# The second matrix of an MLP in seven products of half blocks, in one of three token groups

## The chip, the cores and the metric

The kernel runs on one core of one Trainium2 chip. The metric is the device time of one execution in microseconds (us). Five engines work side by side, each with its own queue of instructions in order, and wait for one another by semaphores: TensorE (PE, matrix products, with PEld for its weight loads), VectorE (DVE), ScalarE (ACT), GpSimd (POOL) and SyncE (SP, which here only issues DMAs; POOL issues DMAs, too).

## The reference

One step of a decoder layer, in float32, for a prompt of 2048 tokens and for 8 samples of 4 tokens:

```
xn  = rms_norm(x, norm_mix_pre);  z = xn @ w_in
y   = concat(mLSTM heads(z), sliding-window attention(z))
x   = x + rms_norm(y @ w_out, norm_mix_post)
u   = rms_norm(x, norm_ffn_pre)
f   = square(relu(u @ w_up)) @ w_down          # 1024 -> 4096 -> 1024
x   = x + rms_norm(f, norm_ffn_post)
x   = x + sigmoid(x @ w_pgate) * (p @ w_pproj)
```

The change concerns `square(relu(u @ w_up)) @ w_down` for a part of the prompt's tokens. The samples' mLSTM and attention ("decode") are a separate piece of work, which reads cached states and keys.

## The kernel before

**Products.** A float32 matrix is held as a pair of tiles, h (rounded) and l (the rest). `mm3` makes a product of three matmuls: h by h, h by l, l by h. Splitting costs a cast on ACT and a subtraction on DVE (`split`) or on DVE and POOL in turn (`wsplit`).

**Groups and steps.** The 16 blocks of 128 tokens form six chunks and three groups of two chunks (`GROUPS`: 6, 6 and 4 blocks). The input projection, the mLSTM and the attention of all blocks come first. Then each group in turn goes through w_out (`mix_mm`, PE name `mo`), the MLP (`mlp`) and the gate (`gate_mm`, `pg` and `pv`). `mlp` cuts the 4096 hidden columns into 16 steps of 256 (FS = 2 halves of 128). Steps 0 and 1 (step 0 alone starts the sums in f) make w_up's product directly (`up`). From step 2 on (`FAST`) `up_both` makes it for both chunks at once in seven products of half blocks instead of eight: it needs sums of the inputs (`sums`, `last_sum`, made during step 1 by DVE and POOL, L1641 to L1675) and differences of the weights (`Ring.product`, L306 to L313), and puts the seven results together on DVE (`add`, L1692). `hidden` then takes relu and square on ACT (L1617, L1618) and splits (L228, L229), giving `hh` and `hl` for each chunk and half.

**w_down.** `down` multiplies the hidden blocks of one chunk with half of w_down's 1024 output columns at a time; a product for one block of tokens takes two halves x three matmuls of 512 columns, in one of three PSUM banks (`ps_mm`, PE name `dn`). DVE adds each finished bank to the sum f in SBUF (L1728). A step has two chunks x two column halves x three blocks: 12 such sums, 72 matmuls. w_up's products go through two other banks (`ps_s`, name `up`).

**The weight ring.** All weight tiles go through one ring of 7 pair tiles (`Ring.pair`, tile name `w`), in the order that `plan` writes out; a tile takes the place of the one seven before it, when that has been used and, if need be, stored. At its first use a weight is loaded raw by SP (`wr`, `wb`), split on ACT (L249) and on DVE or POOL (L250), and, if it is used again, stored in device memory by a DMA that POOL issues (`wk<-w`, L275). Later uses load the stored pair (`w<-wk`, SP). So the first group splits and stores the MLP's weights, and the second and third load them.

**Order.** PE's order is the program's. Side work (decode, transposes, the sums above) is written as generators; each yields a time, and `Flow` continues it when so much matmul time, by its own count, has been written out. `decode` yields `DECW` first, then loads its data through POOL's queue and goes on in pieces between the matmuls of the second group's `mix_mm` and step 0; it is finished (`drain`) before step 1 begins, when its memory on the right side goes to the sums for w_up. The other engines' order is settled by the compiler from the program's order and from what is ready.

## Time and profile before

| what | value |
|---|---|
| runs | 2674.84, 2672.45, 2677.86 us; median 2674.84 |
| profiled execution | 2676.5 us, span in the profile 2674.7 us |
| PE / DVE / ACT / POOL busy | 95% / 55% / 36% / 25% of the span |
| PE's granted clock, mean | 0.981 |
| MLP steps 2 to 13, first group | about 870 to 1267 us of the span |
| MLP steps 2 to 13, second group | about 1600 to 1976 us of the span |
| matmuls of w_down (`dn`) | 1792 with hh, 896 with hl, in all groups |

"Busy" is the time in which an engine works on an instruction. In the chain of work each row is a start, a duration and what ran; in rows of groups, the count follows an x, then come the busy time and the mean in ns of one, and after the second bar the idle time ahead of them with what ended it. In windows, each engine has its busy time and in brackets its count, then come the granted clock, the share of the DMA engines and GB/s. In the order of time, each row is a start, a duration, an engine, a line and an operation.

### The profile page before, as it was taken

The numbers are of one execution on the slowest core, as the hardware profiler recorded it, in microseconds if no ns is written. First come the engines' busy times: TensorE is split into PE (matmuls) and PEld (weight loads), VectorE is DVE, ScalarE is ACT, GpSimd is POOL, SyncE is SP. The second block draws the span as 40 slices with busy tenths as digits, with TensorE's granted clock in tenths as the row PEclk, the third lists the DMA queues.
The fourth block names the chain that finished last, engine by engine and source line by source line (L and its number), as shares of the span: only waits on it lengthen the run. The fifth ranks groups of instructions, "written<-read, shape, count | busy, mean of one in ns | idle before, by whom it ended". The sixth has DMA issues, their size and how long they took to land.

```text
span 2674.7 us, 39114 instructions
## 1 busy us (share of the span) xinstructions
PE 2549.5 (95%) x14260; PEld 2212.9 (83%) x14260; DVE 1481.7 (55%) x3112; ACT 975.9 (36%) x2165; POOL 658.0 (25%) x936
## 2 busy tenths in 40 slices
PE   7899999998899999999998999999999998999998
PEld 6787878877688888888776789988888877999986
DVE  6675666664677655655735564444446345444443
ACT  5545344543455433444513432222223133222231
POOL 5311111111436666666513320000001012000010
PEclk9999999999999999999998999999999998999999
DMA  8765656666786666666987645555557885777786
GB/s 305 268 215 173 217 167 221 210 241 224 255 326 240 254 245 236 236 236 233 341 323 238 209 142 188 189 189 174 173 182 256 288 316 187 254 261 258 257 297 230
DMA packets 215186, 632.23 MB, mean 236 GB/s; under 512 B 24790, under 2 KB 58794, under 8 KB 214977
## 3 DMA queue, kind: packets, MB, share of 16 engines
q1 hardware_dynamic: 169552, 472.19, 52.0%
q0 software_dynamic: 45392, 157.50, 15.1%
q8 instruction: 113, 1.85, 0.3%
q14 instruction: 81, 0.66, 0.1%
q10 hardware_dynamic: 48, 0.03, 0.0%
HBM read 475.47 MB, written 155.25 MB: 236 GB/s over the span
## 4 chain that ended last, share of the span: by engine, by line
PE 74%; DVE 10%; DMA 6%; issue 4%; POOL 3%; ACT 2%; SPq 0%; POOLq 0%; DVEq 0%; ACTq 0%
PE dn L145 20%; PE up L145 20%; PE pg L145 5%; PE mo L145 5%; PE v L145 3%; DMA wk<-w 3%; PE qk L145 2%; DVE hl L229 2%; DMA w<-wk 2%; PE o L145 2%; PE gv L145 2%; PE qa L145 1%; PE aT L149 1%; PE aO L145 1%; PE pv L145 1%
## 5 line engine op out<-in xcount | busy, mean ns | idle before, releaser
L145 PE MATMUL dn<-w,hh 128*128 128x512 f32 x1792 | 566.6, 397 | 13.7 <-DVE f L1449 5.1
L145 PEld LDWEIGHTS dn<-w,hh 128*128 128x128 f32 x1792 | 333.2, 189 | 95.1 <-DVE f L1728 8.6
L1728 DVE TENSOR_TENSOR f<-f,dn 128x512 f32<-128x512 f32 x420 | 286.9, 687 | 222.0 <-PE dn L145 220.9
L145 PE MATMUL dn<-w,hl 128*128 128x512 f32 x896 | 355.5, 397 | 2.5 <-DVE hl L229 2.4
L1692 DVE TENSOR_TENSOR re<-up,re 128x384 f32<-128x384 f32 (+1 forms) x294 | 152.0, 517 | 326.4 <-PE up L145 326.4
L145 PEld LDWEIGHTS dn<-w,hl 128*128 128x128 f32 x896 | 169.0, 189 | 46.3 <-DVE hl L229 7.5
L1693 ACT COPY re<-up 128x384 f32<-128x384 f32 (+1 forms) x42 | 18.9, 450 | 414.8 <-PE up L145 414.8
L1617 ACT ACTIVATE re<-re 128x384 f32<-128x384 f32 (+1 forms) x168 | 83.2, 495 | 207.9 <-DVE re L1692 205.8
L229 DVE TENSOR_TENSOR hl<-re,hh 128x384 fp32r<-128x384 f32 (+1 forms) x192 | 137.7, 717 | 31.1 <-ACT hh L228 30.4
L275 POOL DMA_DIRECT2D wk<-w x242 | 134.0, 555 | 32.2 <-DVE w L250 29.2
L1443 POOL TENSOR_TENSOR f<-f,gffn 128x512 f32<-128x512 f32 x16 | 21.8, 1365 | 476.5 <-ACT j L1441 476.2
L250 POOL TENSOR_TENSOR w<-wr,w 128x512 fp32r<-128x512 f32 (+2 forms) x76 | 104.9, 1380 | 87.5 <-ACT w L249 86.6
L249 ACT CAST w<-wb 128x512 fp32r<-128x512 f32 x98 | 60.7, 621 | 173.2 <-PE dn L145 118.3
L249 ACT CAST w<-wr 128x512 fp32r<-128x512 f32 (+2 forms) x152 | 89.3, 598 | 85.6 <-PE up L145 34.3
L250 POOL TENSOR_TENSOR w<-wb,w 128x512 fp32r<-128x512 f32 x70 | 91.9, 1313 | 116.3 <-ACT w L249 115.8
L1618 ACT ACTIVATE re<-re 128x384 f32<-128x384 f32 (+1 forms) x192 | 95.1, 495 | 5.9
L228 ACT CAST hh<-re 128x384 fp32r<-128x384 f32 (+1 forms) x192 | 92.8, 483 | 6.8
L1043 ACT ACTIVATE s<-s,swt 128x257 f32<-128x257 f32 (+1 forms) x128 | 63.4, 497 | 77.5 <-DVE swt L1040 76.4
L1037 DVE CUSTOM_DVE_ANT_0 s<-aS,cst,sink 128x256 f32<-128x256 f32 (+1 forms) x128 | 57.0, 473 | 59.4 <-PE aS L145 59.2
L1624 POOL CAST hh<-hh 128x16 fp32r<-128x16 f32 x32 | 8.0, 249 | 319.0 <-ACT hh L228 319.0
L145 PE MATMUL up<-t0h,w 128*128 128x384 f32 (+1 forms) x336 | 85.1, 320 | 0.0
L145 PE MATMUL up<-t1h,w 128*128 128x384 f32 (+1 forms) x336 | 85.1, 320 | 0.0
(1537 smaller groups left out, 6530.7 us busy)
## 6 DMA issues: line engine op xcount, KB each, us to landing
w<-wk SPq DMA_DIRECT2D x692, 512.0 KB, 4.7
wk<-w POOLq DMA_DIRECT2D x238, 512.0 KB, 6.6
wr<-in_w_down_dram SPq DMA_DIRECT2D x64, 256.0 KB, 7.7
wb<-in_w_up_dram SPq DMA_DIRECT2D x28, 512.0 KB, 6.8
w<-wk SPq DMA_DIRECT2D x20, 528.0 KB, 4.4
x<-in_x_prompt_dram SPq DMA_DIRECT2D x16, 512.0 KB, 5.2
y<-yd SPq DMA_DIRECT2D x32, 256.0 KB, 7.1
xr<-in_x_prompt_dram SPq DMA_DIRECT2D x16, 512.0 KB, 6.3
```

Source lines behind the costliest of these rows:

```text
L145: ins = self.pe.matmul(out, lhsT, rhs, start=start, stop=stop)
L228: act.copy(hi, src)
L229: dve.tensor_tensor(lo, src, hi.bitcast(F32), ALU.subtract)
L249: act.copy(hi, src)
L250: (eng or weng()).tensor_tensor(lo, src, hi.bitcast(F32), ALU.subtract)
L275: here(put(self.kept[key], t.bitcast(U32)))
L1037: dve.tensor_tensor_reduce(s_[:, s, lo : 2 * P], pS[:, s, lo:], bias[:, j, lo:], 1.0 if s == 0 else 0.0625, sink[:, h : h + 1], ALU.add, A ...
L1043: act.activation(e_, e_, AF.Exp, bias=nm[:, s : s + 1], accum_out=sm[:, s : s + 1])
L1617: act.activation(t, src, AF.Relu)
L1618: act.square(t, t)
L1692: add = lambda out, a, b: dve.tensor_tensor(out, a, b, ALU.add)
L1728: dve.tensor_tensor(out(i), out(i), ps[i], ALU.add)
```

## The change

In the second group (`SGROUP` = 1), steps 2 to 13 (`SEVEN`) go in six pairs. `up_seven` is `up_both` with another end: it names the four hidden blocks A11, A12 (first chunk, halves 1 and 2), A21, A22 (second chunk), and makes on POOL s1 = A21 + A22, s3 = A11 - A21, s2 = s1 - A11 and s4 = A12 - s2. It splits seven operands (A11, A12, A22, s3, s1, s4, s2) instead of four. `down_seven` then makes, for a pair of steps, seven products; in each, a block of 128 tokens sums both steps in one PSUM bank (2 x 3 matmuls), and DVE adds the bank to one or two destinations: quarters of f, or a shared sum U. After the last pair `share` adds U on POOL to three of the four quarters (nine half blocks).

The weights for this are w_down's blocks and four differences of them for each step. They are made in the first group: `Ring.row` with a step collects the four raw blocks, takes four differences on POOL, splits each (ACT and DVE), puts them through the ring and stores them. The second group loads 14 tiles for a pair's w_down instead of 8.

Besides, `DECW` goes from 5 to 20; the raw tiles move to the right side of memory and are given up in the second group's step 1; the pool `wide` (temporaries of the sums for w_up) is given up in step 2 for the operands and U; the pool `sp2` has one buffer instead of two.

```diff
-DECW = 5.0
+DECW = 20.0
...
+SEVEN = range(2, STEPS - 2)
+SGROUP = 1
...
-            self.raw = es.enter_context(tc.tile_pool(name=nm + "raw", bufs=raws))
+            self.raw = es_raw.enter_context(tc.tile_pool(name=nm + "raw", bufs=raws, side="right"))
...
-        def row(self, key, src, n):
+        def row(self, key, src, n, step=None):
             def make(h, l):
                 raw = self.load(n)
                 dma(raw, src)
                 wsplit(h, l, raw)
+                if step is None:
+                    return
+                self.four.append(raw)
+                if len(self.four) < 4:
+                    return
+                b11, b21, b12, b22 = self.four
+                self.four = []
+                sub = lambda out, a, b: pool.tensor_tensor(out, a, b, ALU.subtract)
+                sub(b11, b12, b11)
+                sub(b12, b22, b12)
+                sub(b22, b22, b11)
+                sub(b21, b21, b22)
+                for i, raw in ((1, b11), (3, b12), (2, b22), (4, b21)):
+                    t = self.tile(n)
+                    wsplit(t[:, 0], t[:, 1], raw, dve)
+                    self.keep(("t", step, i), t)
...
+                if gi == SGROUP and s in SEVEN:
+                    if s % 2:
+                        both = s - 1, s
+                        for k in range(FS):
+                            for e in both:
+                                yield row(w_down, e * FS + k, 0)
+                        for i in (3, 4, 1, 0, 2):
+                            for e in both:
+                                yield diff(e, i) if i else row(w_down, e * FS + 1, 1)
+                    continue
+                step = s if gi == 0 and s in SEVEN else None
...
-    sp2 = es2.enter_context(tc.tile_pool(name="sp2", bufs=2, reuse_waits="tile"))
+    sp2 = es2.enter_context(tc.tile_pool(name="sp2", bufs=1, reuse_waits="tile"))
...
+        def up_seven(s, X):
...
+            rectify(t[0], t[0])
+            s1 = wq.tile([P, UW], F32, tag="s1", name=f"s1{nm}")[:, :W]
+            pool.tensor_tensor(s1, t[0], t[2], ALU.add)
+            sub(t[0], t[1], t[0])
+            A["s3"] = parts(hq, t[0], f"{nm}s3")
+            A["s1"] = parts(hq, s1, f"{nm}s1")
+            sub(t[1], s1, t[1])
+            sub(t[3], t[3], t[1])
+            A["s4"] = parts(hq, t[3], f"{nm}s4")
+            A["s2"] = parts(hq, t[1], f"{nm}s2")
+            return A
+
+        def down_seven(s, As, U, first):
+            c0, c1 = chunks
+            def out(ci, half):
+                return lambda i: f[chunks[ci][i]][:, half * 512 : half * 512 + 512]
+            u = lambda i: U[:, i]
+            uses = (
+                ("11", u, out(0, 0)),
+                ("12", out(0, 0)),
+                ("s3", out(1, 1), out(1, 0)),
+                ("22", out(1, 0)),
+                ("s1", out(1, 1), out(0, 1)),
+                ("s4", out(0, 1)),
+                ("s2", u),
+            )
+            for n, (a, *to) in enumerate(uses):
+                w = [[t[:, :512] for t in w] for w in ring.take(2)]
+                for i in range(len(c0)):
+                    ps = psum(ps_mm, f"ds{G}{s}{n}{i}")
+                    for e in range(2):
+                        mm3(ps, [y[:, cols(i)] for y in As[e][a]], w[e], e == 0, e == 1)
+                        pe.tick()
+                    for m, o in enumerate(to):
+                        if first and n == 0 and m == 0:
+                            act.copy(o(i), ps)
+                        else:
+                            dve.tensor_tensor(o(i), o(i), ps, ALU.add)
+
+        def share(U):
+            for ci, half in ((0, 1), (1, 0), (1, 1)):
+                for i, b in enumerate(chunks[ci]):
+                    v = f[b][:, half * 512 : half * 512 + 512]
+                    pool.tensor_tensor(v, v, U[:, i], ALU.add)
...
+            if gi == SGROUP and s in SEVEN:
+                if s == SEVEN[0]:
+                    es_w.close()
...
+                As.append(up_seven(s, X))
+                if len(As) == 2:
+                    down_seven(s, As, U, s == SEVEN[1])
+                    As = []
+                if s == SEVEN[-1]:
+                    share(U)
+                continue
```

More of the change, by code (lines that the diff above doesn't have):

```diff
@@ L281, in get @@
             if key in self.kept:
+                assert all(k != key for _, k, _ in self.later)
                 dma(t.bitcast(U32), self.kept[key])
@@ L386, in hybrid_layer @@
     small = ctx.enter_context(tc.tile_pool(name="small", bufs=6))
-    ring = Ring(ctx, "w", RAWS, PAIRS)
+    es_raw = ExitStack()
+    ring = Ring(ctx, es_raw, "w", RAWS, PAIRS)
     def rows2(k, o, n):
@@ L412, in plan, with row, diff @@
                     )
-        def row(w, k, half):
+        def row(w, k, half, step=None):
             src = w[k * P : (k + 1) * P, half * 512 : half * 512 + 512]
-            return (w.tensor.name, k, half), lambda key: ring.row(key, src, 512)
+            return (w.tensor.name, k, half), lambda key: ring.row(key, src, 512, step)
+        def diff(s, i):
+            return ("t", s, i), lambda key: ring.get(key, 512, None)
         def heads(k, half):
@@ L442, in plan @@
                         yield two(s, q)
+                if gi == SGROUP and s in SEVEN:
[9 more added lines that the diff above has]
+                step = s if gi == 0 and s in SEVEN else None
                 for half in (0, 1, 0, 1) if s == 0 else (0, 1):
                     for k in range(s * FS, (s + 1) * FS):
-                        yield row(w_down, k, half)
+                        yield row(w_down, k, half, step)
             for ci in range(2):
@@ L1612, in up, with parts @@
                 pe.tick()
+        def parts(pool_, t, nm):
+            y = [pool_.tile([P, UW], F32R, tag=f"h{e}", name=f"h{e}{nm}")[:, : t.shape[1]] for e in "hl"]
+            split(*y, t)
+            return y
         def hidden(s, ci, ft, t, src, hid):
@@ L1675, in last_sum, with rectify @@
                 dve.tensor_tensor(l, t3, h.bitcast(F32), ALU.subtract)
-        def up_both(s, X, hid):
+        def rectify(t, src):
+            act.activation(t, src, AF.Relu)
+            act.square(t, t)
+        def up_seven(s, X):
             W = X[0][0].shape[2]
             nm = f"{G}{s}"
+            product = products(s, X)
+            A = {}
+            t = [wq.tile([P, UW], F32, tag="re", name=f"rq{nm}")[:, :W]]
+            t += [wp.tile([P, UW], F32, tag="re", name=f"re{nm}{n}")[:, :W] for n in range(1, 4)]
+            add = lambda out, a, b: dve.tensor_tensor(out, a, b, ALU.add)
+            sub = lambda out, a, b: pool.tensor_tensor(out, a, b, ALU.subtract)
+            act.copy(t[0], product(1))
+            add(t[1], product(2), t[0])
+            rectify(t[1], t[1])
+            A["11"] = parts(hp, t[1], f"{nm}a11")
+            add(t[0], product(6), t[0])
+            add(t[2], product(7), t[0])
+            add(t[3], product(4), t[2])
+            rectify(t[3], t[3])
+            A["12"] = parts(hp, t[3], f"{nm}a12")
+            ps = product(5)
+            add(t[2], ps, t[2])
+            add(t[0], ps, t[0])
+            rectify(t[2], t[2])
+            A["22"] = parts(hp, t[2], f"{nm}a22")
+            add(t[0], product(3), t[0])
+            rectify(t[0], t[0])
[9 more added lines that the diff above has]
+            return A
@@ L1689, in product, with up_both @@
                 return ps
+            return product
+        def up_both(s, X, hid):
+            W = X[0][0].shape[2]
+            nm = f"{G}{s}"
+            product = products(s, X)
             t = [wp.tile([P, UW], F32, tag="re", name=f"re{nm}{n}")[:, :W] for n in range(4)]
@@ L1771, in mlp @@
                 es_lp.close()
+                if gi == SGROUP:
+                    es_raw.close()
                 es_t = ExitStack()
                 tp = es_t.enter_context(tc.tile_pool(name="tp", bufs=1, side="right", reuse_waits="tile"))
[L1774 removed]
+                es_w = ExitStack()
+                ring.wide = es_w.enter_context(tc.tile_pool(name="wide", bufs=WIDE, side="right", reuse_waits="tile"))
                 tsp.add(sums())
+            if gi == SGROUP and s in SEVEN:
+                if s == SEVEN[0]:
+                    es_w.close()
+                    es_w = ExitStack()
+                    hq = es_w.enter_context(tc.tile_pool(name="hq", bufs=6, side="right", reuse_waits="tile"))
+                    wq = es_w.enter_context(tc.tile_pool(name="wq", bufs=2, side="right", reuse_waits="tile"))
+                    U = es_w.enter_context(tc.tile_pool(name="us", bufs=1, side="right", reuse_waits="tile")).tile(
+                        [P, CMAX, 512], F32, name=f"us{G}"
+                    )
+                    As = []
+                As.append(up_seven(s, X))
+                if len(As) == 2:
+                    down_seven(s, As, U, s == SEVEN[1])
+                    As = []
+                if s == SEVEN[-1]:
+                    share(U)
+                continue
             if fast:
```

8 lines of the change are left out of this document (5 added, 3 removed).

## The prediction

> **What bounds the kernel now.** I read the page first, then the chain of work, then windows of one step each, then groups of instructions in the two stretches that the change touches, and last the order of time round single waits.
>
> ```profile
> span 2674.7 us, 39114 instructions
> PE 2549.5 (95%) x14260; PEld 2212.9 (83%) x14260; DVE 1481.7 (55%) x3112; ACT 975.9 (36%) x2165; POOL 658.0 (25%) x936
> ```
>
> TensorE (PE) is the bound as a whole, so fewer matmuls are worth their time wherever PE does not wait already. The chain shows one step of the second group and the distance between two steps of the first; the windows show what the other engines do in such a step.
>
> ```profile
> 1693.73 14.71 PE up L145 x84
> 1708.45 16.72 PE dn L145 x72
> ...
> 1170.89 12.57 PE up L145 x72
> ...
> 1202.89 12.54 PE up L145 x72
> ```
>
> ```profile
> core 0: us, PE busy (x) PEld busy (x) DVE busy (x) ACT busy (x) POOL busy (x), PEclk, DMA share, GB/s
> 1171.00:1203.00 32.00, 31.76 (x158) 28.01 (x157) 19.21 (x28) 13.12 (x25) 20.13 (x23) 1.00 0.64 247
> 1693.73:1725.17 31.44, 31.44 (x158) 28.25 (x157) 14.02 (x23) 6.75 (x13) 0.00 (x0) 1.00 0.57 184
> ```
>
> In the second group a step is 14.71 + 16.72 = 31.4 us, all of it matmul at full clock, with POOL (GpSimd) idle and DVE (VectorE) busy 14.0. There 72 matmuls of w_down take 16.72, so one is 0.232 us, and one of w_up is 14.71 / 84 = 0.175. In the first group the same step takes 1202.89 - 1170.89 = 32.0: PE already loses 0.6, with POOL busy 20.1 and DVE 19.2. These two rows decide the case: the change saves PE time where everything else is idle, and pays with DVE and POOL time where both are busy.
>
> **What the group rows say.** First the stretch 1599 to 2007 (second group), then 883 to 1235 (first group).
>
> ```profile
> L1728 DVE TENSOR_TENSOR f<-f,dn 128x512 f32<-128x512 f32 x156 | 107.4, 688 | 96.3 <-PE dn L145 96.3
> L1692 DVE TENSOR_TENSOR re<-up,re 128x384 f32<-128x384 f32 x91 | 50.7, 557 | 127.6 <-PE up L145 127.6
> L229 DVE TENSOR_TENSOR hl<-re,hh 128x384 fp32r<-128x384 f32 x52 | 28.7, 551 | 2.2 <-ACT hh L228 2.2
> L1618 ACT ACTIVATE re<-re 128x384 f32<-128x384 f32 x52 | 27.4, 526 | 1.6
> L228 ACT CAST hh<-re 128x384 fp32r<-128x384 f32 x52 | 26.8, 515 | 1.7
> ```
>
> ```profile
> L275 POOL DMA_DIRECT2D wk<-w x121 | 66.5, 551 | 16.3 <-DVE w L250 15.8 <-POOL w L250 0.5
> L229 DVE TENSOR_TENSOR hl<-re,hh 128x384 fp32r<-128x384 f32 x44 | 55.9, 1271 | 0.0
> L249 ACT CAST w<-wr 128x512 fp32r<-128x512 f32 x44 | 27.4, 622 | 28.1 <-PE up L145 26.2 <-DMA wk<-w 1.9
> L250 DVE TENSOR_TENSOR w<-wr,w 128x512 fp32r<-128x512 f32 x22 | 15.5, 704 | 2.3 <-ACT w L249 0.6
> L313 POOL TENSOR_TENSOR wb<-wb,wb 128x512 f32<-128x512 f32 x11 | 14.6, 1327 | 16.4 <-DVE w L250 16.4
> L306 POOL TENSOR_TENSOR wb<-wb,wb 128x512 f32<-128x512 f32 x11 | 14.5, 1314 | 1.1 <-DMA wb<-in_w_up_dram 1.1
> ```
>
> The same split of a hidden block (L229) means 0.551 us where POOL is idle and 1.271 where it works. The order of time in one step of the first group says why:
>
> ```profile
> 1119.46 1.31 POOL L307 TENSOR_TENSOR wb<-wb 128x512 f32<-128x512 f32 x1
> 1120.72 1.29 POOL L306 TENSOR_TENSOR wb<-wb,wb 128x512 f32<-128x512 f32 x1
> ```
>
> ```profile
> 1119.85 2.58 DVE L229 TENSOR_TENSOR hl<-re,hh 128x384 fp32r<-128x384 f32 x1
> ```
>
> The DVE split starts inside the first POOL instruction and ends 0.42 after the second, as if it ran only when POOL was through with both. Operations that read PSUM keep their time beside POOL. So a run of POOL instructions holds up a DVE instruction that reads SBUF twice, and everything behind it on DVE.
>
> **The change, part by part.**
>
> *Second group, matmuls.* Six pairs of steps. A pair had 2 x 72 matmuls of w_down and now has 7 products x 3 blocks x 2 steps x 3 = 126: 18 fewer, 108 in all, x 0.232 = -25.1 us. PE has no wait in this stretch, so all of it lies on the path. w_up stays as it is.
>
> *Second group, DVE.* Sums from PSUM grow from 24 to 30 in a pair (+4.1), splits from 8 to 14 (+3.3): 28.0 + 7.4 = 35.4 of some 59. On average it fits; locally it is tight. A product takes PE 18 x 0.232 = 4.18, and one with two destinations takes DVE 6 x 0.688 = 4.13. POOL gets four sums of 128x384 in each step; from 1.31 by width about 1.0 each (an estimate), 3.9 in a run. After the last product of w_up the first new operand (s3) needs a sum (0.56), two activations (1.05), two POOL sums (2.0), a cast (0.52) and a split (0.55): 4.7, or 6.7 if the split waits for POOL's other two. It is used after two products, 8.36 later: hidden, by 1.7. But in those two products DVE has nine sums (6.2), about three splits (1.7) and up to 2.0 of blocking, 9.9 for 8.4, against a cover of two free PSUM banks (2 x 1.39). Ends 0 and 2 us for a pair; nearer to the low one, since products with one destination follow and let DVE catch up: 0.6, x 6 = +3.6. The queue of SP loads 28 tiles for a pair instead of 22, 14.7 MB in 59 us, 250 GB/s, which the windows above show DMA doing in the first group; no cost.
>
> *Second group, the shared sum.* Behind the last pair POOL adds U to nine half blocks.
>
> ```profile
> L1443 POOL TENSOR_TENSOR f<-f,gffn 128x512 f32<-128x512 f32 x16 | 21.8, 1365 | 476.5 <-ACT j L1441 476.2
> ```
>
> 9 x 1.365 = 12.3 us without a break, beside the 14.7 of the next step's w_up; w_down of that step begins after it. A split of that step held up from its start at about 6 until 12.3 keeps the sums behind it, and w_up has two PSUM banks (4.2): ends 0 and 6, I take +3 (the middle; no row shows so long a run).
>
> *First group, twelve steps.* Added in each: four POOL sums (4 x 1.31 = 5.2), four casts on ACT (2.5), four splits on DVE (2.8), four stores issued by POOL (4 x 0.551 = 2.2). POOL goes from 20.1 to 27.5 of 32, DVE from 19.2 to 22.0 before any blocking, stores by 2.1 MB in 32 us, from 247 to about 313 GB/s.
>
> ```profile
> wk<-w POOLq DMA_DIRECT2D x121, 512.0 KB, 7.9
> ```
>
> The four tiles also go through the ring of seven weight tiles. The next step's second tile now takes the place of the third w_down tile, which is free only when the step's last matmul is done; it is wanted one product (12 x 0.175 = 2.1) later, and a cast (0.62) and a split (0.70) need 1.3. Covered by 0.8, unless POOL blocks the split (by 2.0 in the row of 2.58 above). Stores wait in POOL's queue behind its sums, and a tile of the ring is free only when its store has landed, 7.9 after issue; the first w_down tiles take the place of the step's first w_up tiles, stored some 10 us ahead, so this has a cover of about 2. For the sum: below, nothing new reaches PE and a step costs 0.2 more; above, the four POOL sums run without a break, a DVE split waits 5.2 + 0.55, PE's two spare banks cover 2 x 1.39, and a step loses 3.0. A run of two POOL sums goes with the 0.6 lost now; four more make two such runs, so I take 1.1, x 12 = +13.
>
> *Decode starts 15 later.* The waits of PE between 1290 and 1600:
>
> ```profile
> PE dph L149 <- DMA hrow<-in_state_mlstm_conv_dram: 9.0, 1, 9.0
> ...
> PE dn L145 <- ACT hh L228: 2.3, 1, 2.3
> PE dn L145 <- ACT re L1617: 2.3, 1, 2.3
> ```
>
> ```profile
> 1410.00:1420.00 10.00, 6.62 (x26) 5.25 (x27) 5.52 (x22) 1.81 (x3) 5.79 (x10) 0.50 0.26 57
> ```
>
> ```profile
> 1549.02 1.90 PE L145 MATMUL daO<-svc,spts 128*128 128x64 f32 x16
> 1558.28 0.34 PE L145 MATMUL up<-ut10h,w 128*128 128x384 f32 x1
> ```
>
> ```profile
> 1554.59 0.94 DVE L1641 TENSOR_TENSOR ts<-ut11h,ut10h 128x768 f32<-128x768 f32 x1
> ```
>
> Decode's first transposes stand in PE's order before their data: 9.0 of waiting, and a clock of 0.50 behind it: 6.6 us of work at half speed cost about 3 more. Fifteen later in PE's order the data is there if the loads are issued no later: -12. At the other end decode now runs past the start of step 1 (1558.28 against 1549.02 + 15): its last transposes stand without work between them (+1), and the sums for w_up (L1641), which took decode's memory 3.7 us before step 1 began, start about 7 later against PE. They caused the two waits of 2.3; between 0 and 7 more, I take +6 in all. Net -6, between -12 and +3 (loads late, all seven lost).
>
> *Free.* The raw tiles move to the other side of memory and the small pool loses a buffer that the third group uses one at a time; the code shows no wait.
>
> **Sum.** -25.1 + 3.6 + 3 + 13 - 6 = -11.5 against the profiled execution's 2676.5 gives 2665.0; the median of the runs is 1.7 below that execution, so 2663.
>
> **Rivals.** *Slower: POOL in the first group.* Place: the run of four sums and what it does to DVE, with POOL 86% busy. For it: 1.271 against 0.551. Against: stores between the sums let DVE in. At 3.0 a step it is 36 instead of 13: 2686. It decides from (13 + 11.5) / 12 = 2.0 a step.
>
> *Nothing to be seen.* A loss of 2.0 a step in the first group, 24 instead of 13, or the same 11 us lost in the pairs of the second (1.8 each): 2674. For it: DVE with 4.13 in 4.18. Against: its average there is 60%.
>
> *More is kept.* DVE gets in after one POOL instruction instead of after the run. Then no wait exceeds 1.3, the spare banks cover it, the first group pays 0.3 a step (3.6) and the shared sum nothing: 2663 - 9.4 - 3 = 2651. For it:
>
> ```profile
> 1566.90 2.43 POOL L1647 TENSOR_TENSOR ts<-ut11h,ts 128x768 f32<-128x768 f32 x1 [0.96 <-DVE t1l L1659]
> 1569.41 2.44 POOL L1649 TENSOR_TENSOR ts<-ts,ut11l 128x768 f32<-128x768 f32 x1
> ```
>
> ```profile
> 1567.55 2.60 DVE L1659 TENSOR_TENSOR t0l<-ts,t0h 128x768 fp32r<-128x768 f32 x1
> ```
>
> Here the DVE instruction ended at 1570.15, inside the second POOL instruction. Against it: the 2.58 above, where POOL had no gap. [...]
>
> **How the numbers follow.** Forecast 0.46 (own range 2654 to 2669), more kept 0.14, nothing to be seen 0.16, slower 0.24 (the rival 0.20, the rest for a bad decode or DVE). A change under 0.2%, 5.3 us, can't be told from none here. So faster 0.60, same 0.16, slower 0.24. The range from 2646 to 2688 leaves out a tenth at each end: everything kept, and POOL at its worst together with another loss.
>
> **What would show it.** Right: windows of a pair in the second group of 58.7 to 60 instead of 62.8; steps of 33 in the first group with POOL near 27; no wait on hrow; longer waits in step 1. Wrong: waits of PE on f sums or on weights (w) of over 2 us a step in the first group, waits on f sums in the second, or L229 above 2 us in the mean.

## The result and the profile after

Four runs of the changed kernel have a median of 2750.9 us (2744.4 to 2753.7), four of the kernel before on the same chip 2676.4: a ratio of 1.0276, 95% interval 1.0253 to 1.0299. The change costs 2.8%; 2663 was forecast, and the time lies above the range. The profiled execution took 2753.7, its span is 77.2 longer than before's. First the head of the page of the kernel after.

```profile
span 2751.9 us, 39613 instructions
PE 2560.7 (93%) x14152; PEld 2212.2 (80%) x14152; DVE 1602.0 (58%) x3229; ACT 1014.4 (37%) x2252; POOL 807.6 (29%) x1089
```

There are 108 matmuls fewer, and PE is nevertheless busy for 11 us more: behind many waits it runs at a lower clock (0.971 in the mean of the span, 0.981 before). The windows of one step of the first group and one pair of the second:

```profile
core 0: us, PE busy (x) PEld busy (x) DVE busy (x) ACT busy (x) POOL busy (x), PEclk, DMA share, GB/s
1169.20:1206.80 37.60, 34.93 (x163) 29.59 (x161) 25.73 (x32) 15.00 (x29) 28.24 (x30) 0.95 0.72 265
1732.00:1796.93 64.93, 60.55 (x295) 54.05 (x295) 36.33 (x58) 16.17 (x32) 8.53 (x8) 0.97 0.68 226
```

A step of the first group takes 37.6 (32.0 before), with POOL at 28.2 and DVE at 25.7: nothing is full. This pair takes 64.9 (65.2 in the mean of the six, 62.8 before), where the matmuls alone need 58.7. PE's waits, first in the first group's steps (870 to 1310), then in the second's (1660 to 2060); the columns are the total in us, the times, the longest.

```profile
PE up L147 <- ACT w L251: 10.8, 6, 1.8
PE up L147 <- DVE re L1819: 10.1, 5, 3.3
PE dn L147 <- DVE f L1855: 9.2, 10, 1.6
PE dn L147 <- DVE hl L231: 8.2, 4, 4.2
PE up L147 <- POOL w L252: 5.1, 8, 0.7
```

```profile
PE ds L147 <- DVE f L1791: 13.5, 6, 2.2
PE up L147 <- DVE re L1733: 12.8, 6, 2.1
```

From the start of PE's first matmul of each stage, in the order of time, comes the table in which the 77.2 can be placed:

| stage (us) | before | after | difference | forecast |
|---|---|---|---|---|
| first group, steps 2 to 13 | 383.7 | 445.0 | +61.3 | +13 |
| first group, steps 14 and 15 | 75.9 | 80.9 | +5.0 | 0 |
| second group, `mix_mm` (decode's start) | 108.6 | 95.7 | -12.9 | -12 |
| second group, steps 0 and 1 (decode's end) | 92.9 | 104.5 | +11.6 | +6 |
| second group, steps 2 to 13 | 376.8 | 390.9 | +14.1 | -21.5 |
| second group, steps 14 and 15 | 75.7 | 75.6 | -0.1 | +3 |

The rest of the kernel differs by less than 2. Two terms are wrong: the first group by 48, the pairs of the second by 36. Line numbers below are those of the kernel after (L147 matmuls, L231 splits of hidden blocks, L251 and L252 casts and splits of weights, L277 stores, L310 to L316 sums for w_up's weights, L358 the four differences, L1733 and L1791 the second group's sums from PSUM) or, for a variant, of its own text.

### The profile page after: what moved, and what is told of

It reads as the page before. It is cut to its first block, busy times and chain, and to the rows that moved or that the text cites. A ratio compares the mean times of both kernels' runs of the same rounds, so it can differ in the third digit from the quotient of the medians.

```text
span 2751.9 us, 39613 instructions
## 1 busy us (share of the span) xinstructions
PE 2560.7 (93%) x14152; PEld 2212.2 (80%) x14152; DVE 1602.0 (58%) x3229; ACT 1014.4 (37%) x2252; POOL 807.6 (29%) x1089
## 4 chain that ended last, share of the span: by engine, by line
PE 66%; DVE 10%; DMA 7%; POOL 7%; issue 6%; ACT 4%; SPq 0%; POOLq 0%; ACTq 0%; DVEq 0%
PE up L147 16%; PE dn L147 11%; PE ds L147 6%; PE pg L147 5%; PE mo L147 5%; PE v L147 3%; DMA wk<-w 3%; DMA w<-wk 2%; PE qa L147 2%; PE qk L147 2%; POOL w L252 2%; PE gv L147 2%; PE o L147 1%; PE aT L151 1%; PE aO L147 1%
## 5 line engine op out<-in xcount | busy, mean ns | idle before, releaser
L147 PE MATMUL dn<-w,hh 128*128 128x512 f32 x1216 | 392.8, 405 | 28.3 <-DVE f L1855 12.3
L147 PEld LDWEIGHTS dn<-w,hh 128*128 128x128 f32 x1216 | 227.8, 192 | 89.1 <-DVE f L1855 20.9
L147 PE MATMUL dn<-w,hl 128*128 128x512 f32 x608 | 244.1, 401 | 10.3 <-DVE hl L231 10.1
L1855 DVE TENSOR_TENSOR f<-f,dn 128x512 f32<-128x512 f32 x276 | 184.4, 682 | 82.9 <-PE dn L147 82.6
L277 POOL DMA_DIRECT2D wk<-w x290 | 159.3, 551 | 96.2 <-DVE w L252 86.9
L251 ACT CAST w<-wr 128x512 fp32r<-128x512 f32 (+2 forms) x200 | 117.1, 601 | 170.5 <-DMA wk<-w 64.2
L252 DVE TENSOR_TENSOR w<-wr,w 128x512 fp32r<-128x512 f32 (+2 forms) x124 | 129.8, 1064 | 65.7 <-ACT w L251 65.3
L147 PEld LDWEIGHTS dn<-w,hl 128*128 128x128 f32 x608 | 116.6, 192 | 40.8 <-DVE hl L231 13.7
L231 DVE TENSOR_TENSOR hl<-re,hh 128x384 fp32r<-128x384 f32 (+1 forms) x144 | 109.0, 757 | 42.1 <-ACT hh L230 41.2
L252 POOL TENSOR_TENSOR w<-wr,w 128x512 fp32r<-128x512 f32 (+2 forms) x76 | 99.2, 1306 | 90.3 <-ACT w L251 89.5
L1791 DVE TENSOR_TENSOR f<-f,ds 128x512 f32<-128x512 f32 x144 | 94.4, 684 | 39.4 <-PE ds L147 34.7
L1661 ACT ACTIVATE re<-re 128x384 f32<-128x384 f32 (+1 forms) x120 | 57.8, 481 | 154.2 <-DVE re L1819 152.1
L147 PE MATMUL up<-ut01h,w 128*128 128x384 f32 x288 | 88.4, 374 | 23.8 <-ACT w L251 10.8
L252 POOL TENSOR_TENSOR w<-wb,w 128x512 fp32r<-128x512 f32 x70 | 93.4, 1334 | 26.1 <-ACT w L251 25.3
L147 PE MATMUL up<-ut11h,w 128*128 128x384 f32 x288 | 80.9, 343 | 12.8 <-DVE re L1733 12.8
L1081 ACT ACTIVATE s<-s,swt 128x257 f32<-128x257 f32 (+1 forms) x128 | 63.3, 497 | 76.6 <-DVE swt L1078 75.6
L1075 DVE CUSTOM_DVE_ANT_0 s<-aS,cst,sink 128x256 f32<-128x256 f32 (+1 forms) x128 | 57.0, 473 | 59.0 <-PE aS L147 58.7
L147 PE MATMUL up<-t2h,w 128*128 128x384 f32 (+1 forms) x336 | 87.8, 329 | 1.0 <-DVE re L1819 1.0
```

The source lines that it names most:

```text
L147: ins = self.pe.matmul(out, lhsT, rhs, start=start, stop=stop)
L231: dve.tensor_tensor(lo, src, hi.bitcast(F32), ALU.subtract)
L251: act.copy(hi, src)
L252: (eng or weng()).tensor_tensor(lo, src, hi.bitcast(F32), ALU.subtract)
L277: here(put(self.kept[key], t.bitcast(U32)))
L1075: dve.tensor_tensor_reduce(s_[:, s, lo : 2 * P], pS[:, s, lo:], bias[:, j, lo:], 1.0 if s == 0 else 0.0625, sink[:, h : h + 1], ALU.add, A ...
```

## The experiments

In the runs of a part alone the other parts are as in the kernel before. Where the second group works without the first's differences, it loads other tiles of the same size, and its output is then without the differences.

### The three parts alone

First group alone (`up_both` and `down` in the second group, `DECW` 5):

```diff
-                if gi == SGROUP and s in SEVEN:
+                if False:
```

> The first group's part alone: differences made, split and stored, and nobody reads them; the second group and decode as before. Theory A (the loss lies in the first group's own added work): the steps 2 to 15 of the first group take what they take in the changed kernel, 61.3 + 5.0 longer, so 2676 + 66 = 2742, between 2735 and 2748. Rival B (the first group loses because of what the change moves in memory or in decode, not by its added work): under 2700.

2738.5, ratio 1.0239 (1.0212 to 1.0265): theory A. A step takes 36.85.

Second group alone:

```diff
-            return ("t", s, i), lambda key: ring.get(key, 512, None)
+            return row(w_down, s * FS + i % 2, (i - 1) // 2)
...
-                step = s if gi == 0 and s in SEVEN else None
+                step = None
```

> The second group's part alone: no differences are made, and the second group loads the kept tiles of w_down in the places of the differences (the products are then of the wrong weights, in the same number and size). Decode as before. Theory A (the two parts add up, the second group's loss is its own): 2676 + 14 = 2690, between 2683 and 2695, with pairs of 64.9. Rival B (the pairs are slow because POOL's stores of the first group or late differences hold up their loads): pairs of 59 to 60, 2676 - 18 = 2658. Since the raw tiles and the small pool are moved here too, a first group of steps of 32.0 says that the move is free.

2683.8, ratio 1.0031 (1.002 to 1.0043). The pairs take 64.7 in the mean, with the same two waits in each, against 65.2 in the changed kernel: all but 0.5 of their loss is their own. The first group's steps take 31.98, to the hundredth what they took: moving the raw tiles and shrinking the small pool is free.

Decode alone (`DECW = 20.0` in the kernel before):

> The kernel before with decode's first yield at 20 in place of 5, nothing else. Theory A (decode's start and end add up as in the changed kernel: -12.9 in the second group's mix_mm, +11.6 in its steps 0 and 1): 2676 - 1 = 2675, between 2671 and 2679. Rival B (the tail was lengthened by the other parts, and decode alone keeps most of its 12): 2664 to 2668.

2672.0, ratio 0.9989 (0.998 to 0.9998): theory A. `mix_mm` falls by 12.3, steps 0 and 1 grow by 13.5. The three parts add up to 63 + 8 - 4 = 67 of the 75 measured; what the parts cost one another, 8, was not looked into.

### What in the first group costs

Without its sums (the raw blocks are cast, split, put through the ring and stored):

```diff
-                sub(b11, b12, b11)
-                sub(b12, b22, b12)
-                sub(b22, b22, b11)
-                sub(b21, b21, b22)
```

> The first group's part alone, without its four sums on POOL: the four raw blocks themselves are cast, split, put through the ring and stored (what is stored is no difference). Theory A (ring: four more tiles pass through the seven places, and the next step's weights come late): still +45 to +60 against before, 2721 to 2736. Rival B (port: runs of POOL sums hold up the splits on DVE): steps of 32.5 to 33.5, 2676 + 6 to 18 = 2682 to 2694. In between, both have a share.

2694.3, ratio 1.0073 (1.0056 to 1.0089), 33.98 a step: in between.

With the sums on DVE (`dve.` for `pool.` in `sub`):

> The first group's part alone (2738.5, +63), with its four sums on DVE instead of POOL. The part without sums costs 18.6, so the sums stand for 44. Theory A (POOL runs: they hold up DVE's splits and push POOL's own sums and splits of w_up behind them): on DVE each sum takes about 0.7, 2.8 a step, with no instruction blocked for longer than one of its own: 2700 to 2712. Rival B (DVE is short of time, whoever makes the sums, or the raw tiles are held too long): 2730 or more.

2711.3, ratio 1.0137 (1.012 to 1.0155), 35.26 a step: theory A's range, though 17 more than without any sums.

The sums alone, their results dropped:

```diff
-                for i, raw in ((1, b11), (3, b12), (2, b22), (4, b21)):
-                    t = self.tile(n)
-                    wsplit(t[:, 0], t[:, 1], raw, dve)
-                    self.keep(("t", step, i), t)
```

> The first group's part alone, reduced to its four sums on POOL: the results are dropped, with no casts, no splits, no places in the ring and no stores for them. Theory A (the sums' time on POOL is the cost by itself, 44 of the 63): 2676 + 35 to 50 = 2711 to 2726. Rival B (the sums hurt only because the four late splits and the ring's places come on top: each alone has cover): 2676 + 5 to 15 = 2681 to 2691. Prediction's step (two runs of 0.6 a step, 13 in all) would be 2689.

2683.5, ratio 1.0032 (1.002 to 1.0043), 32.82 a step. So a run of POOL sums costs 0.8 a step, where the forecast took 1.1; the cost lies in what they do together with the rest. First guess: four places of the ring one after another, at the end of the step. Spread over the next step's products of w_up:

```diff
+            if i in (0, 1, 4, 5) and self.todo:
+                self.difference()      # one sum on POOL, cast, split, place, store
             return [t.rearrange("p (k n) -> p k n", k=4) for t in v]
```

> The first group's part alone, the same sums, casts, splits, stores and ring places, but not in a run behind the step's last w_down tile: one difference each (a sum on POOL, a cast, a split, a place) behind the first, second, fifth and sixth w_up product of the next step. Theory A (the loss of 63 comes from the run at the step's end: four sums in a row, then four places that nobody multiplies with, so that w_up's first three weights come late): 2676 + 10 to 25 = 2686 to 2701, no waits of PE on w. Rival B (POOL and DVE are short of time together, 28 + 26 of 32 with the locks, wherever the work stands): 2715 to 2740.

2724.3, ratio 1.018 (1.0161 to 1.0198), 35.98 a step. The guess was wrong; only 0.9 of 4.9 goes. Next, everything but the stores (`self.keep(("t", step, i), t)` taken out):

> The first group's part alone (2738.5, +63), without the four stores of the differences; sums on POOL, casts, splits and the four places in the ring stay. Theory A (the stores: POOL issues them behind its sums and behind splits that DVE does late, a place of the ring is free only when its store has landed, ACT's casts of the next weights wait for that, and these make the next splits late): 2676 + 15 to 30 = 2691 to 2706. Rival B (places and splits at the step's end behind a run of sums are enough, stores only ride along): 2725 to 2740.

2704.6, ratio 1.0102 (1.0085 to 1.0119), 34.54. The stores are worth 2.3 a step, half the loss. And stores without places and splits, from the raw tiles:

```diff
-                for i, raw in ((1, b11), (3, b12), (2, b22), (4, b21)):
-                    t = self.tile(n)
-                    wsplit(t[:, 0], t[:, 1], raw, dve)
-                    self.keep(("t", step, i), t)
+                for i, out in ((1, b11), (3, b12), (2, b22), (4, b21)):
+                    self.keep(("t", step, i), out)
```

> The first group's part alone, its four sums on POOL in a run as in the change, but the differences are stored as they are, 256 KB each from the raw tiles, with no cast, no split and no place in the ring. Theory A (the ring's places, held by stores, make the difference between 7.6 for the sums alone and 63): 2676 + 8 to 15 = 2684 to 2691. Rival B (four more DMA issues in POOL's queue behind the sums make the other stores late, too): 2700 to 2715.

2684.8, ratio 1.0035 (1.0023 to 1.0046), 32.79: no more than the sums alone. The same with the second and fourth sum on DVE:

> As the differences stored raw, with the second and the fourth sum on DVE. Theory A (a run of four POOL sums holds up DVE's splits): with runs of one, 2676 + 2 to 8 = 2678 to 2684, faster than the kernel before it. Rival B (no gain from shorter runs, DVE pays what POOL saves): equal or slower by up to 5.

2689.7, ratio 1.0052 (1.0037 to 1.0067), 33.26. Theory A failed: shorter runs on POOL gain nothing, and DVE pays. Last, casts, splits and places with neither sums nor stores:

> The first group's part alone, without its sums and without its stores: the raw blocks are cast, split on DVE and put into four places of the ring, and nothing more. The table so far: sums 7.6; casts, splits, places and stores without sums 18.6; sums, casts, splits and places without stores 30; all of them 63. Theory A (the sums make the splits late, and the late splits the places): alone, casts, splits and places cost 0 to 8, 2676 to 2684. Rival B (casts, splits and places are the cost with or without sums): 15 to 25, 2691 to 2701.

2667.7, ratio 0.9968 (0.9954 to 0.9981), 31.36: below the range of theory A, too (2676 to 2684), and better than before by 0.6 a step, its whole loss. So the table of a step in us, each against 31.98:

| | no stores | stored |
|---|---|---|
| sums alone | +0.84 | +0.81 (raw) |
| casts, splits, places | -0.62 | +2.00 |
| sums, casts, splits, places | +2.56 | +4.87 |

Sums by themselves cost 0.8, casts, splits and places less than nothing. Together they cost 2.3 more than the two apart (2.56 - 0.84 + 0.62). Stores cost nothing from raw tiles, and 2.6 (without sums) or 2.3 (with them) from places in the ring. What stands behind the two interactions is read in the order of time. Sums with splits, in the kernel without stores:

```profile
1178.94 4.58 POOL L358 TENSOR_TENSOR wr<-wr,wr 128x512 f32<-128x512 f32 x3
```

```profile
1179.78 0.88 DVE L231 TENSOR_TENSOR hl<-re,hh 128x384 fp32r<-128x384 f32 x1 [0.92 <-ACT hh L230]
1180.58 0.55 DVE L1818 TENSOR_TENSOR re<-up,re 128x384 f32<-128x384 f32 x1
1181.05 1.32 DVE L252 TENSOR_TENSOR w<-wr,w 128x512 fp32r<-128x512 f32 x1
1182.29 0.55 DVE L1818 TENSOR_TENSOR re<-up,re 128x384 f32<-128x384 f32 x1
1182.76 1.18 DVE L231 TENSOR_TENSOR hl<-re,hh 128x384 fp32r<-128x384 f32 x1
1183.86 1.89 DVE L252 TENSOR_TENSOR w<-wr,w 128x512 fp32r<-128x512 f32 x3
1185.67 0.68 DVE L1854 TENSOR_TENSOR f<-f,dn 128x512 f32<-128x512 f32 x1
```

```profile
1186.39 0.74 PE L147 MATMUL dn<-w,hh 128*128 128x512 f32 x2 [1.89 <-DVE f L1854]
```

During POOL's run DVE's splits take 0.9 to 1.3 instead of 0.55 to 0.7 (what the expectations call port and locks shows itself in such longer times alone; what makes them no run shows), and when the run ends at 1183.5 three splits of differences (1.89) stand in DVE's queue ahead of the sum that empties a bank. PE has used its three banks and waits for 1.89. In this variant these waits are nearly all there is from 870 to 1300; where the sums are left out, too, PE waits for nothing there but one transpose:

```profile
PE dn L147 <- DVE f L1854: 25.2, 12, 4.8
```

The stores with the places, in the changed kernel, with rows of ACT and DVE, then POOL, ACT and PE:

```profile
1181.41 0.62 ACT L251 CAST w<-wr 128x512 fp32r<-128x512 f32 x1 [6.73 <-issue]
1182.06 0.69 DVE L252 TENSOR_TENSOR w<-wr,w 128x512 fp32r<-128x512 f32 x1 [0.71 <-ACT w L251]
```

```profile
1176.85 1.73 POOL L277 DMA_DIRECT2D wk<-w  x3 [1.04 <-DVE w L252]
1183.05 1.73 POOL L277 DMA_DIRECT2D wk<-w  x3 [4.46 <-DVE w L252]
1184.80 1.30 POOL L310 TENSOR_TENSOR wb<-wb 128x512 f32<-128x512 f32 x1
1186.80 1.30 POOL L316 TENSOR_TENSOR wb<-wb,wb 128x512 f32<-128x512 f32 x1 [0.70 <-DVE w L252]
...
1192.60 1.26 POOL L314 TENSOR_TENSOR wb<-wb,wb 128x512 f32<-128x512 f32 x1
```

```profile
1193.90 1.66 ACT L251 CAST w<-wb 128x512 fp32r<-128x512 f32 x3 [1.18 <-POOL wb L314]
```

```profile
1194.57 0.58 PE L147 MATMUL up<-ut01h,w 128*128 128x384 f32 x1 [1.80 <-ACT w L251]
1195.92 1.01 PE L147 MATMUL up<-ut01h,w 128*128 128x384 f32 x2 [0.45 <-POOL w L252]
```

The fourth difference takes the place of the step's first w_down tile (seven tiles before it), and PE uses that until the last block of w_down's third quarter, at 1181.3. ACT's cast stands still for 6.73. The trace names no releaser for it here, but in the step before it names PE, at the same point of w_down:

```profile
1143.78 0.62 ACT L251 CAST w<-wr 128x512 fp32r<-128x512 f32 x1 [5.56 <-PE dn L147]
```

DVE's split follows, and POOL, which has come to that difference's store, stands for 4.46 with the sums for w_up's weights behind it. L310, L316 and L314 then come one after another, and the third product of w_up finds its weight 1.80 and then 0.45 late, and starts at a lower clock, 0.50 from 1194.71 to 1198.13: 1.01 for two matmuls that take 0.51 later in the step. The group rows say how long POOL's stores stand in all: from 870 to 1310 in the changed kernel, and from 870 to 1250 in the one that stores raw differences (the pairs' stores; its raw ones stand 0.0) and in the one with places alone:

```profile
L277 POOL DMA_DIRECT2D wk<-w x176 | 95.8, 546 | 78.4 <-DVE w L252 73.7 <-issue 2.3 <-ACT re L1662 1.1
```

```profile
L277 POOL DMA_DIRECT2D wk<-w x129 | 71.2, 553 | 1.0 <-issue 1.0
```

```profile
L277 POOL DMA_DIRECT2D wk<-w x134 | 73.6, 551 | 81.8 <-issue 79.5 <-DVE w L252 1.7 <-POOL w L252 0.5
```

The last row bounds what this shows: with places alone POOL's stores stand as long, and PE waits for nothing. What counts is when such a wait ends. There L310 runs 5.9 after w_down's first matmul (1184.85 against 1179.00), in the step above 15.8 after it (1184.80 against 1169.04).

Nor is it the only way in which stores and places cost time. Without the sums, where stores cost 2.6, PE never waits for a weight in these steps (870 to 1250), but for DVE's sums from PSUM, and ACT's casts wait for places whose stores have not landed:

```profile
PE dn L147 <- DVE f L1850: 21.3, 23, 1.9
ACT w L251 <- DMA wk<-w: 65.0, 42, 3.3
```

The late casts make DVE's splits late (DVE waits 33.3 for them), and these stand ahead of the sums that empty the banks. Before the change ACT waits 3.2 for landings, in the changed kernel 73.2 (870 to 1310): both ways are found there, and how its 2.3 divides between them is not shown. In the spread variant the waits for landings are the longest (870 to 1250):

```profile
ACT w L251 <- DMA wk<-w: 101.2, 27, 6.3
```

### What in the second group costs

The rows of a pair in the changed kernel, PE and then DVE:

```profile
1755.09 0.44 PE L147 MATMUL up<-ut11h,w 128*128 128x384 f32 x1 [2.14 <-DVE re L1733]
...
1771.55 1.22 PE L147 MATMUL ds<-w,hh14a 128*128 128x512 f32 x2 [2.24 <-DVE f L1791]
```

```profile
1751.15 0.93 DVE L231 TENSOR_TENSOR hl14s<-rq,hh14s 128x384 fp32r<-128x384 f32 x1 [3.43 <-ACT hh14s L230]
1752.01 1.37 DVE L231 TENSOR_TENSOR hl14s<-s,hh14s 128x384 fp32r<-128x384 f32 x1
1753.54 1.03 DVE L231 TENSOR_TENSOR hl14s<-re,hh14s 128x384 fp32r<-128x384 f32 x2 [0.16 <-ACT hh14s L230]
1754.48 0.55 DVE L1733 TENSOR_TENSOR re<-up,rq 128x384 f32<-128x384 f32 x1
...
1768.23 0.94 DVE L231 TENSOR_TENSOR hl15s<-rq,hh15s 128x384 fp32r<-128x384 f32 x1 [0.99 <-ACT hh15s L230]
1769.08 1.35 DVE L231 TENSOR_TENSOR hl15s<-s,hh15s 128x384 fp32r<-128x384 f32 x1
1770.35 0.55 DVE L231 TENSOR_TENSOR hl15a<-re,hh15a 128x384 fp32r<-128x384 f32 x1
1770.82 0.67 DVE L1791 TENSOR_TENSOR f<-f,ds 128x512 f32<-128x512 f32 x1
```

DVE idles 3.43 for a cast that waits for POOL's sums, makes four splits that nobody needs for some microseconds, and only then empties the bank that PE waits for. The same happens in w_down. The compiler's order puts these splits first. Two variants change the order alone. The first writes the splits of s3, s1, s4, s2 behind the next sums from PSUM, on DVE only:

```diff
-            A["s3"] = parts(hq, t[0], f"{nm}s3")      # and s1, s4, s2
+            late.extend([(A, "s3", t[0], f"{nm}s3"), ...])
...
+            due(1)                                     # split what is late
             add(t[0], product(6), t[0])
...
+                        here(dve.tensor_tensor(o(i), o(i), ps, ALU.add))
+                due((1, 1, 2, 0, 0, 0, 0)[n]) if i == len(c0) - 1 else None
```

> The second group's part alone (kept tiles in the places of the differences; 2683.8), with DVE's order changed and nothing else: the splits of the four sums s3, s1, s4, s2 stand behind the sums from PSUM that PE needs, in the next step's w_up products or between the products of w_down. Same instructions, same counts. Theory A (order of DVE's queue: splits fed by POOL stand ahead of the sums from PSUM): both waits of a pair (2.1 and 2.2) and the slow clock behind them go, pairs of 59 to 60.5 instead of 65: 2684 - 27 to -36 = 2648 to 2657. Rival B (DVE and POOL lack time or lock each other out wherever the splits stand): the waits move elsewhere, pairs of 63 to 65, 2675 to 2684.

2702.8, ratio 1.0101 (1.0074 to 1.0127), pairs of 67.6: worse than both theories. DVE's rows show why; the queue that holds it up is now ACT's, where the casts fed by POOL still stood ahead of the rectifying:

```profile
1753.70 0.51 ACT L1732 CAST hh16s<-re 128x384 fp32r<-128x384 f32 x1 [1.26 <-POOL re L1744]
1754.12 0.52 ACT L1722 ACTIVATE re<-re 128x384 f32<-128x384 f32 x1
```

```profile
1756.04 0.56 DVE L231 TENSOR_TENSOR hl17a<-re,hh17a 128x384 fp32r<-128x384 f32 x1 [5.00 <-ACT hh17a L230]
```

The second variant writes out ACT's order, too (`here` around each cast, `Relu` and square), and splits the odd step's A22 between the first products of w_down, as its buffer is free only then:

```diff
-            act.activation(t, src, AF.Relu)
-            act.square(t, t)
+            here(act.activation(t, src, AF.Relu))
+            here(act.square(t, t))
...
+            if s % 2 == 0:
                 A["22"] = parts_here(hp, t[2], f"{nm}a22")
...
+            if s % 2:
+                late.append((A, "22", hp, t[2], f"{nm}a22"))
```

> The second group's part alone, with the order of DVE and of ACT written out: casts and splits of s3, s1, s4, s2 stand behind the next products' sums from PSUM on both queues, and the odd step's fourth hidden block is split between w_down's first products, where its buffer is free. Same instructions. In the kernel with late splits on DVE alone, the casts fed by POOL still stood ahead of the rectifying on ACT. Theory A (order of both queues): pairs of 59 to 60.5, 2676 - 13 to -23 = 2653 to 2663. Rival B (lack of time on DVE in w_down's first products): pairs of 62 to 65, 2670 to 2684.

2654.9, ratio 0.9912 (0.9891 to 0.9933), pairs of 59.1: theory A. Of PE's waits from 1590 to 1960 this is left:

```profile
PE up L147 <- DVE rq L1747: 1.8, 6, 0.3
```

With the four sums on DVE as well (`here(dve.` for `pool.`):

> As the second group ordered, with the four sums s1, s3, s2, s4 of each step on DVE, too, POOL idle. Theory A (the order was the matter, POOL's sums run long but off the path): equal to the kernel before it within 3. Rival B (POOL's sums still hold up splits): faster by 3 to 10. Rival C (DVE is short): slower by 3 or more.

2664.5, ratio 0.9952 (0.9937 to 0.9967), pairs of 60.7: rival C.

### Decode, and the whole repaired

Before's kernel with decode's start later and its end where it was:

```diff
-DECW = 5.0
+DECW = 14.0
...
-        yield 10.0
+        yield 1.0
```

> The kernel before with decode's first yield at 14 in place of 5 and its later yield of 10 at 1: decode's start is 9 later, what comes after the gates is where it was. Theory A (two separate effects: the wait on hrow at the front, the late end at the tail): the front gives 12, the tail nothing, 2676 - 9 to -13 = 2663 to 2667. Rival B (with the short pause PE stands before the transposes of the gates' result, or the end is late all the same): 2671 to 2677, as with the first yield alone (2672).

2664.0, ratio 0.9965 (0.995 to 0.9979): theory A by the time. The stages of its profiled execution (2668.3) show only a part of it: steps 0 and 1 take 92.4, as before, and the wait on hrow falls from 9.0 to 1.6, but `mix_mm` falls by 3.9 only, with a stretch of 13.7 at a clock of 0.50 that begins at 1464.0.

Differences spread, second group ordered, decode as here:

> The whole change with the three repairs together: differences spread over the next step's w_up products, the second group's DVE and ACT order written out, decode's first yield at 14 with the later 10 at 1. If the three add up and each theory A holds: 2676 + 10 to 25 - 13 to -23 - 12 = 2651 to 2676, against 2664 for the kernel before with decode's yields alone. With rivals B in the first group: 2690 or more.

2702.3, ratio 1.0093 (1.0062 to 1.0125): rival B. The pairs take 59.1, the first group's steps 36.05.

Differences stored raw, and split in the second group:

```diff
+        def difference(self, key):
+            t = self.tile(512)
+            self.store()
+            h, l = t[:, 0], t[:, 1]
+            dma(l.bitcast(U32), self.kept[key])
+            act.copy(h, l.bitcast(F32))
+            dve.tensor_tensor(l, l.bitcast(F32), h.bitcast(F32), ALU.subtract)
+            return h, l
```

> The whole change with repairs: differences stored raw in the first group (sums on POOL) and loaded raw into the ring in the second, where ACT casts and DVE splits them (16 instructions more in a pair); the second group's order written out; decode's first yield 14, its later one 1. If the parts add up: 2676 + 8 to 15 - 21 - 12 + 0 to 10 = 2651 to 2668, against 2664 for the kernel before with decode's yields alone. If the casts and splits of weights in DVE's and ACT's queues cost the pairs what the order had won (2 to 4 a pair): 2670 to 2680.

2656.8, ratio 0.9935 (0.9914 to 0.9956): the parts add up. The pairs take 60.2 in the mean. DVE's queue holds these splits up, and PE waits for w. With that last subtraction on POOL (`pool.` for `dve.`):

> As the whole change with raw differences (2656.8), but in the second group POOL, not DVE, takes the second half of the split of a loaded difference. The pairs there take 60.6 instead of 59.1, with PE waiting on DVE's splits of w. Theory A (DVE's queue holds these splits up): pairs of 59.1 to 60, 2648 to 2655. Rival B (POOL's instructions of 1.3 stand ahead of the sums s1 and s3 and lock DVE out): pairs of 61 or more, 2658 or more.

2650.6, ratio 0.9898 (0.988 to 0.9917), pairs of 59.1: theory A. This version beats both kernels. Its pair, with POOL now at 19.0 of 59.0 and PE without a gap, and its page's head:

```profile
1740.00:1799.00 59.00, 58.69 (x295) 52.73 (x294) 35.12 (x59) 20.59 (x40) 18.99 (x16) 1.00 0.64 214
```

```profile
span 2644.0 us, 39596 instructions
```

Its stages against before: first group's steps 2 to 13 +7.4, second group's -22.1, `mix_mm` -14.0, steps 0 and 1 +0.5. So 7.4 - 22.1 = -14.7 is what the seven products bring; the rest is decode's move, which needs none of them and alone, as above, was worth 11.9.

## Why the prediction was wrong, point by point

**Matmuls, -25.1: right.** Once the order of the queues lets PE run, a pair falls from 62.8 to 59.1, 22.1 in all; the 0.5 a pair that is missing goes partly with the wait of 0.3 that is left.

**Stalls of the second group, +3.6 (0.6 a pair): wrong, +36 (6.0 a pair, against the ordered pairs' 59.1).** The step that failed is "hidden, by 1.7". It asked whether s3 is ready when PE needs it, and s3 is: split at 1769.2, used from 1776.0. It did not ask what stands behind the splits on DVE, whose order is not the order of need. The count for w_down's first products, 9.9 us of work against 8.4 and the spare banks, had named the place and had 2 as its upper end, although its own cover of 2 x 1.39 exceeds the 1.5 by which 9.9 is more than 8.4; 2.24 was measured, and taking the low end was the error. The other wait, in the next step's w_up, where there are two banks, is missing altogether. The windows behind the two waits give the clock:

```profile
1755.09:1758.80 3.71, 3.71 (x21) 3.71 (x22) 1.67 (x3) 1.54 (x3) 0.00 (x0) 1.00 0.34 85
1771.55:1775.30 3.75, 3.75 (x10) 2.99 (x10) 2.43 (x4) 0.00 (x0) 0.00 (x0) 0.54 0.02 9
```

In this pair 2.14 + 2.24 of waiting and 3.75 x 0.46 = 1.7 of slow clock behind the second wait are the 6.

**First group, +13 (1.1 a step): wrong, +61 (5.1).** The run of sums, for which 1.1 stood, costs 0.8 by itself. What failed are two covers. "PE's two spare banks cover" held for the sums, not for sums with three late splits queued behind them (+2.3). And "the first w_down tiles take the place of the step's first w_up tiles, stored some 10 us ahead, so this has a cover of about 2" looked at the wrong tile: the fourth difference waits for a w_down tile that is in use, and its store makes POOL wait with w_up's sums behind it; besides, casts wait for places whose stores have not landed, 73.2 instead of 3.2 (+2.3 for both). The text had the sentence "stores wait in POOL's queue behind its sums", but not its reverse, sums behind stores.

**The rival "POOL in the first group"** had the right sign and engine, 3.0 a step as its price, and the run as its mechanism. The run alone does not do it; 5.1 is above the end taken for the range. **"More is kept"**, by which DVE gets in after one instruction of POOL, is what the rows of the variant without stores show: inside POOL's run of 4.58, which ends at 1183.52, DVE finished the splits of 0.88 and 1.32, and the one of 1.18 ended 0.42 behind it. There the rows speak for the rival, against the forecast's "through with both". Others do not. In the changed kernel one split spans four instructions of POOL, with a store between the first two:

```profile
1050.14 5.72 DVE L252 TENSOR_TENSOR w<-wr,w 128x512 fp32r<-128x512 f32 x1 [1.71 <-ACT w L251]
```

So both occur, and what decides between them was not tested. Where DVE did get in, as in the variant without stores, the time was lost all the same, to the queues. Two more sentences of the forecast bear on this. "Stores between the sums let DVE in" has rows for and against it: in before's trace a split that began inside an instruction of POOL took 0.95 (1115.88 to 1116.83) and ended 0.56 after it, beside stores, while the split of 5.72 did not end at the store. "Operations that read PSUM keep their time beside POOL" has its figures in before's rows, 883 to 1235 against 1599 to 2007: 554 ns against 557 for w_up's sums (L1692), 685 against 688 for w_down's (L1728).

**Shared sum, +3: nothing.** All nine POOL sums ran in one stretch of 11.6 us (2054.5 to 2066.1; 12.3 forecast), most of it beside w_up of step 14, which begins at 2056.3, and steps 14 and 15 took 75.6, 75.7 before.

**Decode, -6: -1.3 and, alone, -3.8 of the median.** The front is right (-12 forecast, -12.9 and -12.3 measured), the tail was put at 6 and is 11.6 to 13.5. Front and tail are separate: with the delay taken out again behind the gates, in the last variant, `mix_mm` takes 14.0 less, and steps 0 and 1 0.5 more.

**Free:** right for the raw tiles and the small pool.

## What to carry to other kernels

An average of 60% on an engine says little: list, for each in-order queue, what stands ahead of the instruction on which the bottleneck waits, and what that in turn waits for, through every engine (POOL, ACT, DVE); mend one queue only, and the wait moves to the next, as the late splits showed (67.6 a pair instead of 64.7, with DVE waiting 5.00 for a cast). An instruction that issues a DMA is a wait like any other for what stands behind it (POOL's store stood 4.46 ahead of w_up's sums). Of two additions one cost 0.8 a step alone and the other nothing, and together they cost 2.3 more than that, so try parts in pairs before they are added up.

## What was not expected of the hardware

- In the variant with casts, splits and places alone, 373 DVE instructions where before had 322 (870 to 1250), PE lost nothing at all: the splits of hidden blocks took 0.599 us instead of 1.242, near the 0.551 that they take where POOL is idle. That they no longer fell into POOL's sums, and that this phase between two engines was worth the 0.6 a step, more work notwithstanding, is the author's reading of these times.
- Moving two of four sums from POOL to DVE made the step longer by 0.5, moving the second group's four sums a step made the pair longer by 1.6, though POOL needs 1.02 for what takes DVE 0.56: DVE's queue is the one that PE waits for (12.8 and 13.5 in the changed kernel's pairs).
- Two waits of nearly the same length in one pair, 2.14 and 2.24, were followed by a clock of 1.00 and of 0.54 (the two windows above). What parts them is where they lie. In the changed kernel's trace all stretches at half clock begin on one grid of 3.41 us. The wait of 2.14 (1752.95 to 1755.09) lies across a boundary of this grid, the wait of 2.24 (1769.31 to 1771.55) within one of its windows, and from the next boundary on the clock is 0.50 (1771.57 to 1774.98):

```profile
1751.09:1754.50 3.41, 1.86 (x11) 1.54 (x9) 3.19 (x5) 1.37 (x4) 1.79 (x2) 1.00 0.69 217
1768.16:1771.57 3.41, 1.17 (x6) 0.59 (x5) 3.34 (x5) 0.86 (x3) 1.78 (x2) 1.00 0.86 298
```

In the steps of both groups (870 to 1310 and 1660 to 2060) every full-clock window of the grid with PE busy for 1.62 or less was followed by half clock, and none with 1.70 or more. The wait of 1.80 before 1194.57 is of the first kind (busy 1.61 from 1191.30 to 1194.71); a wait of 3.25 (1012.10 to 1015.35) is parted into 1.70 and 1.87 of busy time, and the clock stays at 1.00. The first pair's wait of 2.14 (1686.46 to 1688.60) fell within a window (busy 1.27 from 1686.24 to 1689.65), and half clock followed there, too. So in these steps the clock fell behind windows in which PE was idle for 1.79 of 3.41 or more, a little over half, and half clock lasted one window or two (3.41 or 6.83).

What stays open: how the 2.3 of stores and places divides between POOL's queue and the places whose stores have not landed; which place the fourth difference takes where it does not wait for PE (without sums its cast waits 1.38 for a landing, at 1176.48, without stores for POOL's sum only, although by the ring's order it is the same place); when a waiting DVE split gets in between two instructions of POOL; and the loss of 2.3 from sums and splits was not taken further apart by engine.
